# The recurrence's values, the forget gates and the first two heads' queries and keys by Strassen's method, and the forget gates' chain on 64 partitions

## The chip, the core and the metric

The kernel runs on one core of a Trainium2 chip. That core has five engines with queues of their own: TensorE (PE, with its weight loads shown apart as PEld), VectorE (DVE), ScalarE (ACT), GpSimd (POOL) and SyncE (SP), which here issues all transfers. The metric is the time of one execution in microseconds (us); lower is better. The profile is of one execution, and its span runs from the first to the last instruction.

## The reference, cut to what matters

One encoder layer on x of 1024 rows by 1024 features, all in float32:

```python
proj = x @ w_in                      # 1024 x (3*512 + 8 + 4*512 + 2*1024)
q_a, k_a, v_a, f_a, q_b, f_b, i_b, g_b, gate_a, gate_b = split(proj)
log_f = log_sigmoid(f_a + b_f)       # 8 heads; F = cumsum over rows
y_a = fox_attention(...)             # softmax(q k / 8 + F[t] - F[s], s <= t) v, 8 heads of 64
y_b = hgrn2_chunkwise(q_b, 1 - f, i_b, log f)   # 4 heads of 128, state carried over rows
y = sigmoid(gate_a) * (y_a @ w_pa) + sigmoid(gate_b) * (norm(y_b) * ... @ w_pb)
x1 = layer_norm(ALPHA * x + y @ w_o)
out = layer_norm(ALPHA * x1 + swiglu(x1 @ w_ff_in) @ w_ff_out)
```

The change concerns three products with x: `i_b` (the recurrence's values, 512 columns) together with `f_a` (the eight forget gates, 8 columns), and the columns of `q_a` and `k_a` that belong to heads 0 and 1 (128 columns each). It also concerns the cumulative sums of the log forget gates, which every score needs.

## The kernel before, in words

All numbers are float32, and TensorE is given each operand as a high and a low part: ACT casts the high part (`split`: `act.copy`), DVE subtracts it from the source for the low part, and three matmuls (hi·hi, hi·lo, lo·hi: `mm3`) make one product. x is kept transposed, with features on partitions, as four tiles `xh0`, `xh1`, `xl0`, `xl1`. A dot product over 1024 features is eight steps of 128, so 24 matmuls.

The work comes in this order (`Plan` below): the attention's values `va` (the eight PSUM banks hold eight blocks of 128 rows); the recurrence's values with the forget gates, `vb_acc` (eight row blocks, each in two halves of 260 columns, `HV`, so 16 accumulations of 24 matmuls of 260 columns, 384 in all); a transpose of the forget gates (`fps`), a chain of small DVE and ACT steps on 8 partitions by 1024 rows (`fz`, `fa`, `fe`, `fu`: log-sigmoid, then a scan along the rows, then the sums of the odd blocks turned round, since the rows of every second block lie in reverse order); the first pair of heads' queries and keys (`qps`, `kps`, 96 matmuls of 512 columns), whose parts `q2`, `k2`, `kl` ACT and DVE write; and then attention for four pairs of heads, the recurrence's four heads (`bps` and others), the gates, the branch projections `pps`, the output projection `o`, and the feed-forward network (`fa`, `fb`, `fc`, `p`). The box of a head, `box`, holds the cumulative sums of all rows in every partition. It is loaded from `nf_d` in DRAM, POOL adds the causal mask to parts of it, and DVE adds it to the scores `s` while it takes the row maxima (`p<-s,box`).

The order is not that of the code. Each engine call is recorded in `Plan`, a list scheduler with a cost for each call (`Plan.cost`) places the calls one at a time by earliest start and then by rank, and `Plan.issue` sends them out in that order; all instructions therefore bear the line of `getattr(q.engine, method)` in `Plan.issue` (L280). Tiles are slots of a tag with a fixed number of buffers (`BUFS`), handed out first come, first served, so a call also waits for a slot. The gates' plain products (`gps`, weights `wg`, the first eight blocks, `PLAIN`) depend on x alone and are put between other matmuls wherever TensorE would stand still; the remaining gate blocks (`gs`) already use Strassen's method, as does the feed-forward network.

Of the kernel before, what the change touches and what calls it, by code (L numbers as in the profile page):

```python
# [16 lines left out]
P = 128  # L17
# [4 lines left out]
HA, DH = 8, 64  # L22
HB = 4
# [260 lines left out]
def trunk(ctx: ExitStack, tc, a: dict, out: bass.AP):  # L284
# [36 lines left out]
    def const(name, shape, dt=F32):  # L321
        t = keep(shape, name, dt)
        sync.dma_start(t, a[name])
        return t
# [9 lines left out]
    def f(ap):  # L334
        return ap.bitcast(F32)
# [50 lines left out]
    stage = ["qk"] * 6 + ["kb"] * 2  # L386
# [3 lines left out]
    for c2 in range(KC // 2):  # L390
        raws = []
        wraw = take("pf", [2, NB], f"wva{c2}_r")
        for j in range(2):
            raw = full(stage[2 * c2 + j], f"x{2 * c2 + j}_r")
# [25 lines left out]
    causal = const("causal", [P, 2, P], BF16)  # L420
    bf = const("bf", [HA, 1])


    box1 = take("m", [4, S], "box1")
    NV = NB + HA
    HV = NV // 2
    wv = []
    for c in range(KC):
        raw = raw_load(a["w_vb"][c], [NV], f"wvb{c}")
        hi, lo = (full(WTAGS[2 * c + j], f"wvb{c}_{'hl'[j]}", F32R)[:, :NV] for j in range(2))  # L430
        split(hi, lo, raw)
        wv.append((hi, lo))
    vb_d = dram.tile([NT, P, NB], F32, name="vb_d")
    ft = take("gt", [NT, HA], "ft")
    for t in range(NT):
        vb = half(("tt", "ph")[t % 2], f"vb{t}")
        o = [bank(("pt", "h")[t % 2], f"vb_acc{t}_{i}")[:, :HV] for i in range(2)]
        for i in range(2):
            r = slice(i * HV, (i + 1) * HV)
            for c in range(KC):  # L440
                h, l = X(c)
                mm3(o[i], h[:, blk(t)], l[:, blk(t)], wv[c][0][:, r], wv[c][1][:, r], c == 0, c == KC - 1)
        act.copy(vb[:, :HV], o[0])
        dve.tensor_copy(vb[:, HV:], o[1][:, :NB - HV])
        dve.tensor_copy(ft[:, t, :], o[1][:, NB - HV:])
        sync.dma_start(vb_d[t], vb)

    fz, fa, fe, fu = (full("pf", n)[:HA] for n in ("fz", "fa", "fe", "fu"))
# [6 lines left out]
    dve.tensor_scalar(fa, fz, bf, 0.0, op0=ALU.add, op1=ALU.min)  # L455
# [8 lines left out]
    nf = box1[:HA, 2, :]  # L464
    dve.tensor_tensor_scan(nf, fz, fa, 0.0, op0=ALU.add, op1=ALU.subtract)

    nfv, fzv = (t.rearrange("p (j c t) -> p j c t", c=2, t=P) for t in (nf, fz))
    odd = fzv[:, :, 1, :]
    ends = [nfv[:, :, c, P - 1:P].to_broadcast([HA, 4, P]) for c in range(2)]
    dve.tensor_sub(odd[:, :, 1:], ends[1][:, :, 1:], nfv[:, :, 1, :P - 1])  # L470
    dve.tensor_sub(odd[:, :, 0:1], nfv[:, :, 1, P - 1:P], nfv[:, :, 0, P - 1:P])
    dve.tensor_add(nfv[:, :, 1, :], odd, ends[0])
    nf_d = dram.tile([HA, S], F32, name="nf_d")
    sync.dma_start(nf_d, nf)
# [3 lines left out]

    def qk_project(p):
        q2 = [full("qk", f"q2_{p}_{i}", F32R) for i in range(2)]  # L480
        k2 = [full("kb", f"k2_{p}_{i}", F32R) for i in range(2)]
        kl = [full("qk", f"kl_{p}_{i}", F32R) for i in range(2)]
        for b in range(2):
            w = weights(a["w_qk"][b, p], [KC, P], f"w{'qk'[b]}{p}", 0)
            for hf in range(2):
                o = bank("s" if p == 0 else "g", f"{'qk'[b]}ps{p}_{hf}")
                project(o, w, hf)
                for i in range(2):
                    me, ot = slice(i * DH, (i + 1) * DH), slice((1 - i) * DH, (2 - i) * DH)
                    if b == 0:  # L490
                        act.activation(q2[i][me, hs(hf)], o[me], AF.Copy, scale=0.125)
                        dve.scalar_tensor_tensor(q2[i][ot, hs(hf)], o[me], 0.125, f(q2[i])[me, hs(hf)],
                                                 op0=ALU.mult, op1=ALU.subtract)
                    else:
                        act.copy(k2[i][me, hs(hf)], o[me])
                        act.copy(k2[i][ot, hs(hf)], o[me])
                        dve.tensor_sub(kl[i][me, hs(hf)], o[me], f(k2[i])[me, hs(hf)])
                        act.copy(kl[i][ot, hs(hf)], f(kl[i])[me, hs(hf)])
        return q2, k2, kl

    def attention(p, qk):
        q2, k2, kl = qk
        for i in range(2):
# [4 lines left out]
            sync.dma_start(nfx[:, :, 1, :], nf_d[h].rearrange("(j t) -> j t", t=P).partition_broadcast(P))  # L508
# [9 lines left out]
            for qb in range(NT):  # L518
                n = (qb + 1) * P
                pt = full("pf", f"p{h}_{qb}") if qb > 3 else half("ph", f"p{h}_{qb}")  # L520
                mx = small([P, 3], "mx")
# [20 lines left out]
                nm = small([P, 1], "nm")  # L542
# [6 lines left out]
                sm = small([P, 1], "sm")  # L549
                act.activation(pt[:, :n], pt[:, :n], AF.Exp, bias=nm, scale=1.0, accum_out=sm)  # L550
                rs = small([P, 1], "rs")
# [30 lines left out]
    lmask = const("lmask", [P, 2, P], U16)  # L582
# [30 lines left out]
    def hgrn(h, qfg, box):  # L613
# [127 lines left out]
        for hf in range(2):  # L741
            op = bank("pv", f"op{h}_{hf}")
            ss = small([P, 4], "ss")
# [9 lines left out]
            rr = small([P, 4], "rr")  # L753
# [24 lines left out]
    qk = qk_project(0)  # L778
# [16 lines left out]

    def operand4(tags, name):
        ts = [[take(tags[2 * j + i], [2, NB], f"{name}{'hl'[i]}{j}", F32R) for j in range(2)] for i in range(2)]
        return [[ts[i][c // 2][:, c % 2, :] for c in range(4)] for i in range(2)]
# [650 lines left out]
```

## Time and profile before

| what | value |
|---|---|
| time, median of 3 runs | 1476.8 us (1476.67 to 1477.74) |
| profiled execution | 1476.22 us |
| its span | 1474.4 us |
| mean clock granted to TensorE | 0.998 |
| PE, PEld, DVE, ACT, POOL busy | 1455.1, 1208.2, 1053.3, 659.8, 96.6 us |

In the views of the profile a row such as `L280 PE MATMUL vb_acc<-wvb_l,xh 128*128 128x260 f32 x128 | 36.0, 281 | 0.0` stands for 128 matmuls into `vb_acc` of 260 columns: 36.0 us busy in all, 281 ns each, and no idle time before them. Matmuls overlap in the pipeline, so the distance from one start to the next is shorter than the length of one. A row of the timeline gives the start, the length, the engine, the line, the operation and, in brackets, how long the engine had stood idle before and what it waited for. A row of the table by windows gives, for a stretch of time, its length and then the busy time (and number of instructions) of PE, PEld, DVE, ACT and POOL, the granted clock, the share of the DMA engines' time and GB/s.

### The profile page before, as it was taken

How to read it: one execution, taken by the hardware profiler on the slowest of the kernel's cores; microseconds unless marked ns; L12 is line 12 of the kernel's file. 1: busy time of each engine (PE TensorE's matmuls, PEld its weight loads, DVE VectorE, ACT ScalarE, POOL GpSimd, SP SyncE). 2: the span in 40 equal slices, each digit the busy share in tenths (PEclk: the TensorE clock that was granted, in tenths of full speed). 3: DMA queues.
4: the chain of work that ended last, by engine and by line, in shares of the span. 5: the costliest groups of instructions: out<-in, count | busy, mean ns of one | idle time of the engine just before them, and what ended most of it. 6: DMA issues, size and time to landing. Idle time of an engine off the chain costs nothing.

```text
span 1474.4 us, 19347 instructions
## 1 busy us (share of the span) xinstructions
PE 1455.1 (99%) x7033; PEld 1208.2 (82%) x7033; DVE 1053.3 (71%) x1993; ACT 659.8 (45%) x1121; POOL 96.6 (7%) x116
## 2 busy tenths in 40 slices
PE   9999999999999999999999899999999999999998
PEld 7997888888887888788888788888888888888887
DVE  5237676686887899645848897676666666798597
ACT  5126667577568566234611443333333333534430
POOL 0004142130101000000001000000000000000000
PEclk9999999999999999999999999999999999999999
DMA  6202222121211235347610314232222335976741
GB/s 237 78 37 83 58 66 72 47 76 39 73 44 58 86 134 178 119 155 253 225 45 0 115 35 143 100 99 95 95 98 102 107 108 179 342 264 225 258 159 58
DMA packets 79566, 174.86 MB, mean 119 GB/s; under 512 B 7528, under 2 KB 20456, under 8 KB 79472
## 3 DMA queue, kind: packets, MB, share of 16 engines
q1 hardware_dynamic: 79472, 173.64, 34.9%
q8 instruction: 55, 0.90, 0.2%
q14 instruction: 39, 0.32, 0.1%
HBM read 134.52 MB, written 39.09 MB: 118 GB/s over the span
## 4 chain that ended last, share of the span: by engine, by line
PE 93%; DVE 4%; ACT 1%; DMA 1%; issue 0%; POOL 0%; SPq 0%; DVEq 0%; ACTq 0%; POOLq 0%
PE p L280 14%; PE fb L280 11%; PE fc L280 8%; PE fa L280 8%; PE bps L280 8%; PE pps L280 6%; PE o L280 6%; PE gs L280 5%; PE gps L280 5%; PE vb_acc L280 3%; PE va_acc L280 3%; PE kps L280 3%; PE pv L280 2%; PE s L280 2%; PE qps L280 2%; PE pt L280 2%
## 5 line engine op out<-in xcount | busy, mean ns | idle before, releaser
L280 PE MATMUL p<-dp 128*128 128x512 f32 (+1 forms) x957 | 210.0, 382 | 0.0
L280 PEld LDWEIGHTS p<-dp 128*128 128x128 f32 x957 | 175.3, 188 | 34.8
L280 PE MATMUL fc<-xs,Tp 128*128 128x512 f32 x528 | 127.0, 389 | 0.0
L280 PE MATMUL fb<-xs,Tp 128*128 128x512 f32 x528 | 126.7, 389 | 0.0
L280 PE MATMUL fa<-x,Tp 128*128 128x512 f32 x480 | 115.7, 389 | 0.3 <-DVE u L280 0.3
L280 PEld LDWEIGHTS fb<-xs,Tp 128*128 128x128 f32 x528 | 99.1, 188 | 20.6
L280 PEld LDWEIGHTS fc<-xs,Tp 128*128 128x128 f32 x528 | 99.0, 188 | 20.7 <-ACT xs L280 0.2
L280 ACT CAST Tp<-t 128x512 fp32r<-128x512 f32 x88 | 54.3, 620 | 116.2 <-PE fc L280 71.9
L280 PEld LDWEIGHTS fa<-x,Tp 128*128 128x128 f32 x480 | 90.0, 188 | 19.3 <-ACT p L280 0.7
L280 DVE TENSOR_TENSOR Tp<-t,Tp 128x512 fp32r<-128x512 f32 x88 | 60.6, 691 | 60.5 <-ACT Tp L280 60.0
L280 ACT CAST dp<-dap 128x1024 fp32r<-128x1024 f32 (+1 forms) x42 | 41.1, 982 | 99.3 <-PE p L280 45.3
L280 PE MATMUL bps<-xh,wb_l 128*128 128x512 f32 x192 | 76.0, 396 | 0.0
L280 PE MATMUL bps<-xh,wb_h 128*128 128x512 f32 x192 | 75.9, 395 | 0.0
L280 PE MATMUL bps<-xl,wb_h 128*128 128x512 f32 x192 | 75.9, 396 | 0.0
L280 POOL TENSOR_TENSOR rstd<-ve,mhalf 128x1 f32<-128x1 f32 x16 | 14.9, 932 | 887.4 <-DVE ve L280 887.4
L280 DVE TENSOR_TENSOR tl<-pt,th 128x512 fp32r<-128x512 f32 (+1 forms) x96 | 50.7, 552 | 20.3 <-ACT th L280 20.0
L280 DVE TENSOR_TENSOR dp<-dap,dp 128x1024 fp32r<-128x1024 f32 (+1 forms) x42 | 47.5, 1134 | 15.4 <-ACT dp L280 15.4
L280 PE MATMUL fb<-x,Tp 128*128 128x512 f32 x240 | 57.7, 389 | 0.0
L280 POOL TENSOR_SCALAR p<-p,rs 128x128 f32<-128x128 f32 (+3 forms) x64 | 47.5, 749 | 140.7 <-DVE rs L280 91.0
L280 ACT CAST th<-pt 128x512 fp32r<-128x512 f32 (+1 forms) x96 | 43.2, 479 | 28.3 <-PE pt L280 27.1
L280 ACT ACTIVATE p<-p,nm 128x128 f32<-128x128 f32 (+3 forms) x64 | 49.5, 776 | 9.0 <-DVE nm L280 8.5
L280 PEld LDWEIGHTS fb<-x,Tp 128*128 128x128 f32 x240 | 45.1, 188 | 9.4
(374 smaller groups left out, 3511.5 us busy)
## 6 DMA issues: line engine op xcount, KB each, us to landing
dbp<-in_w_fo SPq DMA_DIRECT2D x45, 512.0 KB, 4.8
dap<-a_d SPq DMA_DIRECT2D x35, 512.0 KB, 4.8
a_d<-ar SPq DMA_DIRECT2D x42, 256.0 KB, 3.7
wu_r<-in_w_ff SPq DMA_DIRECT2D x20, 512.0 KB, 3.6
wg_r<-in_w_ff SPq DMA_DIRECT2D x20, 512.0 KB, 3.6
a_d<-as SPq DMA_DIRECT2D x33, 256.0 KB, 2.4
wg_r<-in_w_g SPq DMA_DIRECT2D x16, 512.0 KB, 3.6
sg<-gate_d SPq DMA_DIRECT2D x32, 256.0 KB, 3.5
```

What stands on the lines that cost most here:

```text
L280: getattr(q.engine, method)(*args, **kw)
```

## The change

Strassen's method in Winograd's form multiplies two matrices that are cut in quarters with seven products of quarters instead of eight, and pays with sums of quarters ahead of and behind the products. The change applies it in two places, with the same sums of x (`vops`) in both. With a11, a21 the first 512 features of rows 0 to 511 and of rows 512 to 1023, and a12, a22 the same for the last 512 features, they are p7: a11−a21, p5: a21+a22, p6: p5−a11, p3: a12−p6.

* **Sums of x** (`winograd_sums`). Four sums of four tiles 128x512, on DVE in place in the raw x tiles, and a split of each: 16 sums and 16 subtractions on DVE, 16 casts on ACT. The raw x0 to x3 lie in one tile (`x03_r`, tag "m"), x4 to x7 in "qk".
* **Recurrence's values and forget gates** (`vb_mul`). Seven products into eight banks (`vbx0` to `vbx3`, `vby0` to `vby3`), each of four row blocks, four steps and three matmuls of 260 columns: 336 matmuls. The weights come as four tiles of 128x1040 (`wvb0` to `wvb3`). DVE makes four sums of them, and each product's weights are split as two pieces of 520 columns (`Tvp…`), 14 splits in place of 8. Behind the products stand eight ACT copies and 20 DVE adds of 260 columns into `vbt`, and two DVE copies that gather `ft`. The eight stores `vb_d` go out in pieces of 1 KB per row.
* **Queries and keys of heads 0 and 1** (`qk_first`). Seven products of 12 matmuls of 512 columns (84), on three banks (`qk0_s`, `qk0_pt`, `qk0_s`). The weights are loaded raw (`wq0_r`, `wk0_r`), DVE makes four sums and six combinations of 128x512, ACT two copies, and there are seven splits of 128x512 (`Tqk…`) in place of four. The other three pairs are as before.
* **Forget gates' chain.** One transpose gives `fps` of 64 partitions (block and head) by 128 rows. The chain of steps is the same on 64x128 in place of 8x1024; the sums of the blocks before come from one matmul of one column, `fbase`, with the constant matrix `before`. `nf_d` is now stored by block and head, and the box is loaded from it with another pattern.
* **Tiles.** To make room, the small tiles of the softmax (`mx`, `nm`, `sm`, `rs`) become columns of one, as do two of the recurrence (`ss`, `rr`) and three of the layer norms (`mv`, `ve`, `rstd`), and the masks `causal` and `lmask` take turns in one tile.

```diff
@@ trunk: x raws, sums of x
-    stage = ["qk"] * 6 + ["kb"] * 2
+    xraw = take("m", [4, S], "x03_r")
+    xraws = [xraw[:, c, :] for c in range(4)]
...
+    def sums4(op, dst, x, y, sub):
+        for c in range(4):
+            (dve.tensor_sub if sub else dve.tensor_add)(dst[c], x[c], y[c])
+            split(op[0][c], op[1][c], dst[c])
+
+    vops = {"p1": quarter(0, 0), "p2": quarter(1, 0), "p4": quarter(1, 1)}
+
+    def winograd_sums(ops, raws, tiles):
+        a11, a21, a12, a22 = ([x[:, hs(m)] for x in raws[4 * j:4 * j + 4]] for j, m in ((0, 0), (0, 1), (1, 0), (1, 1)))
+        for name, tile, dst, x, y, sub in (("p7", tiles[2], a11, a11, a21, True), ("p5", tiles[0], a21, a21, a22, False),
+                                           ("p6", tiles[1], a22, a22, a11, True), ("p3", tiles[3], a12, a12, a22, True)):
+            ops[name] = tile()
+            sums4(ops[name], dst, x, y, sub)
@@ trunk: recurrence's values and forget gates
-    for t in range(NT):
-        vb = half(("tt", "ph")[t % 2], f"vb{t}")
-        o = [bank(("pt", "h")[t % 2], f"vb_acc{t}_{i}")[:, :HV] for i in range(2)]
-        for i in range(2):
...
-                mm3(o[i], h[:, blk(t)], l[:, blk(t)], wv[c][0][:, r], wv[c][1][:, r], c == 0, c == KC - 1)
...
+    def vb_mul(p, src, o, first):
+        lane = lane_of(None)
+        T = [[take(f"w{x}{lane}", [2, HV], f"Tv{p}{x}{j}", F32R) for j in range(2)] for x in "hl"]
+        for j in range(2):
+            split(T[0][j], T[1][j], src[:, 2 * j:2 * j + 2])
...
+        for t in range(4):
+            for c in range(4):
+                mm3(o[t][:, :HV], A[0][c][:, blk(t)], A[1][c][:, blk(t)], T[0][c // 2][:, c % 2], T[1][c // 2][:, c % 2],
+                    first and c == 0, c == 3, more)
...
+    vb_mul("p1", b11, vx, True)
+    for t in range(4):
+        act.copy(p1v[:, t], vx[t][:, :HV])
+    vb_mul("p2", b21, vx, False)
+    vb_out(0, 0, act.copy, vx)
+    dve.tensor_sub(b12, b12, b11)
+    dve.tensor_sub(t2, b22, b12)
+    vb_mul("p6", t2, vy, True)
+    vb_out(0, 1, dve.tensor_add, vy, p1v)
+    vb_mul("p5", b12, vx, True)
...
+    vb_mul("p3", b22, vx, False)
+    vb_out(1, 0, dve.tensor_add, vy, p1v)
...
@@ trunk: forget gates' chain
-    for hf in range(2):
-        fps = bank("s", f"fps{hf}")
-        for t in range(4):
-            tr(fps[:HA, blk(t)], ft[:, 4 * hf + t, :], ident)
-        dve.tensor_copy(fz[:, hs(hf)], fps[:HA])
-    act.activation(fe, fz, AF.Abs, bias=bf, scale=1.0)
+    fps = bank("h", "fps")[:BH, :P]
+    tr(fps, ft.rearrange("p t h -> p (t h)"), ident)
+    f4 = half("gt", "f4")[:BH]
+    fz, fa, fe, fu = (f4[:, blk(i)] for i in range(4))
+    act.activation(fe, fps, AF.Abs, bias=bf, scale=1.0)
...
+    base = bank("h", "fbase")[:BH, :1]
+    mm(base, before[:, :BH], nf[:, P - 1:P], start=True, stop=True)
+    dve.tensor_sub(fz, fz, fa)
+    dve.tensor_scalar(fz, fz, before[:, BH + 1:BH + 2], base, op0=ALU.mult, op1=ALU.add)
+    dve.scalar_tensor_tensor(nf, nf, before[:, BH:BH + 1], fz, op0=ALU.mult, op1=ALU.add)
+    nf_d = dram.tile([NT, HA, P], F32, name="nf_d")
...
@@ qk_first, called in place of qk_project(0)
+        def mul(p, src, o, first):
+            T = [take(f"w{x}0", [4, P], f"Tqk{p}{x}", F32R) for x in "hl"]
+            split(*T, src)
+            more = {} if first else {"skip_group_check": True}
+            for c in range(4):
+                mm3(o, T[0][:, c], T[1][:, c], vops[p][0][c], vops[p][1][c], first and c == 0, c == 3, more)
+
+        mul("p1", b11, oa, True)
+        act.copy(p1, oa)
+        mul("p2", b21, oa, False)
+        dve.tensor_sub(b12, b12, b11)
+        dve.tensor_sub(t2, b22, b12)
+        qk_heads(0, 0, oa, *tiles)
+        mul("p6", t2, ob, True)
+        dve.tensor_add(u2, ob, p1)
+        mul("p5", b12, oc, True)
...
```

The planner sets the new order. On TensorE, at the end of the recurrence's values, there stands before (`vb_acc7_1` is the second half of the last row block, `qps0_0` the first half of the queries):

```order
L280 MATMUL vb_acc7_1_161<-wvb7_l_135,xh1_67 128x260
L280 MATMUL vb_acc7_1_161<-wvb7_h_134,xl1_69 128x260
L280 MATMUL fps0_166<-ident_108,ft_137 8x128 x4
L280 MATMUL fps1_167<-ident_108,ft_137 8x128 x3
L280 MATMUL qps0_0_190<-xh0_66,wq0_h0_186 128x512
L280 MATMUL fps1_167<-ident_108,ft_137 8x128
L280 MATMUL qps0_0_190<-xl0_68,wq0_h0_186 128x512
L280 MATMUL qps0_0_190<-xh0_66,wq0_l0_187 128x512
```

and in the changed kernel (`vbx3` is the last bank of product p3, `gps0_0_0` a plain gate product):

```order
L281 MATMUL vbx3_138<-Tvp3l1_170,vs4h3_121 128x260
L281 MATMUL vbx3_138<-Tvp3h1_168,vs4l3_125 128x260
L281 MATMUL gps0_0_0_1120<-xh0_66,wg0_0_h0_1116 128x512
L281 MATMUL gps0_0_0_1120<-xl0_68,wg0_0_h0_1116 128x512
L281 MATMUL qk0_s_191<-xh0_66,Tqkp1h_200 128x512
L281 MATMUL qk0_s_191<-xl0_68,Tqkp1h_200 128x512
L281 MATMUL gps0_0_0_1120<-xh0_66,wg0_0_l0_1117 128x512
L281 MATMUL qk0_s_191<-xh0_66,Tqkp1l_201 128x512
```

Gate products that stood behind the queries and keys now stand between them, and the one transpose stands eight rows further on, no longer right behind the recurrence's values.

On DVE, at the end of the attention's values, there stands before (`wvb…_l` are the low parts of the recurrence's weights, `wq0_l…` those of the first queries, and the copies take the finished banks of `va`):

```order
L280 TENSOR_TENSOR wvb5_l_129<-wvb5_r_127,wvb5_h_128 128x520
L280 TENSOR_TENSOR wvb6_l_132<-wvb6_r_130,wvb6_h_131 128x520
L280 TENSOR_TENSOR wvb7_l_135<-wvb7_r_133,wvb7_h_134 128x520
L280 TENSOR_TENSOR wq0_l0_187<-wq0_r_185,wq0_h0_186 128x512
L280 TENSOR_TENSOR wq0_l1_189<-wq0_r_185,wq0_h1_188 128x512
L280 COPY va_107<-va_acc0_71 128x512
L280 TENSOR_TENSOR wg0_0_l0_1302<-wg0_0_r_1300,wg0_0_h0_1301 128x512
L280 COPY va_107<-va_acc2_73 128x512
```

and in the changed kernel (`x4_r` to `x7_r` hold the sums by then, `vs4` is the operand of p3, `Tvp1` the weights of p1):

```order
L281 TENSOR_TENSOR vs4l2_124<-x6_r_98,vs4h2_120 128x512
L281 TENSOR_TENSOR x7_r_99<-x7_r_99 128x512
L281 TENSOR_TENSOR Tvp1l0_145<-wvb0_r_128,Tvp1h0_143 128x520
L281 TENSOR_TENSOR wvb1_r_129<-wvb1_r_129,wvb0_r_128 128x1040
L281 TENSOR_TENSOR vs4l3_125<-x7_r_99,vs4h3_121 128x512
L281 TENSOR_TENSOR Tvp1l1_146<-wvb0_r_128,Tvp1h1_144 128x520
L281 TENSOR_TENSOR lbt_182<-lbl_181 128x4
L281 RECIPROCAL lbt_182<-lbt_182 128x4
L281 TENSOR_TENSOR lbt_182<-lbt_182 128x4 x2
L281 TENSOR_SCALAR lbt_182<-lbt_182 128x4
L281 COPY va_104<-va_acc0_72 128x512
```

All sums of x and their low parts now stand ahead of the first bank's copy, and the splits of the recurrence's weights, but for those of p1, behind it.

On DVE, in the stretch of the first queries and keys, there stands before (`f…` are the steps of the forget gates' chain, `q2` the scaled queries, `wk0_l0` a low part of the keys' weights):

```order
L280 TENSOR_SCALAR fu_165<-fe_164 8x1024
L280 TENSOR_SCALAR fu_165<-fu_165 8x1024
L280 SCALAR_TENSOR_TENSOR q2_0_0_179<-qps0_0_190,q2_0_0_179 64x512
L280 TENSOR_TENSOR fe_164<-fe_164,fu_165 8x1024
L280 SCALAR_TENSOR_TENSOR q2_0_1_180<-qps0_0_190,q2_0_1_180 64x512
L280 TENSOR_TENSOR fe_164<-fe_164,fu_165 8x1024
L280 TENSOR_TENSOR wk0_l0_194<-wk0_r_192,wk0_h0_193 128x512
L280 TENSOR_TENSOR fz_162<-fz_162,fe_164 8x1024
```

and in the changed kernel (`f4` is the chain's tile, `Tqk…l` the low parts of the products' weights, `wq0_r` and `wqk_t2` sums of weights):

```order
L281 TENSOR_TENSOR Tqkp2l_203<-wq0_r_186,Tqkp2h_202 128x512
L281 COPY ft_127<-vbt_134 128x8x4
L281 TENSOR_TENSOR wq0_r_186<-wqk_t2_188,wq0_r_186 128x512
L281 COPY ft_127<-vbt_134 128x8x4
L281 TENSOR_TENSOR wq0_r_186<-wq0_r_186,wqk_t2_188 128x512
L281 TENSOR_SCALAR f4_173<-fps_172,bf_107 64x128
L281 TENSOR_SCALAR f4_173<-f4_173 64x128
L281 TENSOR_TENSOR Tqkp6l_205<-wqk_t2_188,Tqkp6h_204 128x512
L281 TENSOR_SCALAR f4_173<-f4_173 64x128
L281 TENSOR_TENSOR f4_173<-f4_173 64x128
L281 TENSOR_TENSOR wg0_0_l1_1119<-wg0_0_r_1115,wg0_0_h1_1118 128x512
```

The chain's steps now stand between weight sums and splits of the seven products, no longer between the queries' evacuations.

More of the change, by code (lines that the diff above doesn't have):

```diff
@@ L22 @@
 HA, DH = 8, 64
+HV = 260
 HB = 4
@@ L419, in trunk @@
     ident = const("ident", [P, P])
[L420 to L432, printed above, removed]
+    causal = const("causal", [P, 2, P], BF16, "mask")
+    bf = const("bf", [NT * HA, 1])
@@ new lines, in quarter @@
+    def quarter(i, m):
+        return [[x[i][:, c, hs(m)] for c in range(4)] for x in (xh, xl)]
+    def sums4(op, dst, x, y, sub):
[9 more added lines that the diff above has]
+            sums4(ops[name], dst, x, y, sub)
@@ L485, in qk_project @@
             for hf in range(2):
-                o = bank("s" if p == 0 else "g", f"{'qk'[b]}ps{p}_{hf}")
+                o = bank("g", f"{'qk'[b]}ps{p}_{hf}")
                 project(o, w, hf)
[L488 to L498, printed above, removed]
```

166 lines of the change are left out of this document (114 added, 52 removed).

## The prediction

> **What bounds the kernel now.** I read the page's shares first, then the chain that ended last.
>
> ```profile
> span 1474.4 us, 19347 instructions
> PE 1455.1 (99%) x7033; PEld 1208.2 (82%) x7033; DVE 1053.3 (71%) x1993; ACT 659.8 (45%) x1121; POOL 96.6 (7%) x116
> PE 93%; DVE 4%; ACT 1%; DMA 1%; issue 0%; POOL 0%; SPq 0%; DVEq 0%; ACTq 0%; POOLq 0%
> ...
> 8.13 41.78 PE va_acc L280 x183
> 49.91 45.55 PE vb_acc L280 x384
> ...
> 224.99 10.88 PE kps L280 x48
> ```
>
> TensorE carries 93% of the chain, and the whole of the recurrence's values is one piece of it. Since a busy TensorE need not run at its pace, I take the pace from pieces: 384 matmuls of 260 columns in 45.53 us (next table) are 118.6 ns each, 48 of 512 columns in 10.88 us are 226.7 ns. So a matmul removed there is worth its full pace, provided that TensorE is given other work without a gap. The stages show who could be late instead.
>
> ```profile
> core 0: us, PE busy (x) PEld busy (x) DVE busy (x) ACT busy (x) POOL busy (x), PEclk, DMA share, GB/s
> 8.13:49.75 41.62, 41.62 (x184) 34.47 (x184) 23.50 (x34) 20.77 (x31) 0.00 (x0) 1.00 0.58 198
> 49.75:95.28 45.53, 45.53 (x385) 45.51 (x384) 4.35 (x16) 4.12 (x10) 0.00 (x0) 1.00 0.15 53
> 95.28:97.06 1.78, 1.78 (x14) 1.42 (x12) 1.57 (x4) 1.14 (x2) 0.00 (x0) 1.00 0.15 58
> 97.06:114.08 17.02, 15.45 (x68) 12.13 (x66) 13.89 (x18) 7.78 (x10) 0.00 (x0) 1.00 0.03 11
> 114.08:120.44 6.36, 6.36 (x29) 5.32 (x30) 2.04 (x4) 3.59 (x7) 0.00 (x0) 1.00 0.45 147
> 120.44:300.00 179.56, 179.38 (x944) 146.42 (x943) 128.10 (x452) 124.62 (x267) 54.58 (x66) 1.00 0.22 65
> 300.00:571.25 271.25, 268.46 (x1428) 224.17 (x1428) 223.91 (x503) 182.97 (x325) 26.95 (x30) 1.00 0.24 78
> ```
>
> The first row is the attention's values (DVE idle 18 of 42 us), the second the recurrence's (DVE and ACT all but idle), the third to fifth the transposes and the first queries and keys (TensorE 1.6 us short, DVE at 82% in the middle one), the last two attention and recurrence. The clock is full throughout, so no term needs a correction for it. Two waits matter:
>
> ```profile
> PE fa L280 <- ACT Tp_0h L280: 4.1, 1, 4.1
> ...
> PE kps L280 <- DVE wk_l L280: 1.6, 2, 1.3
> ```
>
> The first lies in the feed-forward network, where the change alters nothing. The second is a key-weight split held up in DVE's queue behind the forget gates' chain on 8 partitions; below I count it as removed.
>
> **The change part by part, TensorE.** The recurrence's values fall from 384 to 7·4·4·3 = 336 matmuls: 48·118.6 ns = −5.69 us. Queries and keys of the first pair fall from 96 to 84: 12·226.7 ns = −2.72 us. The transposes:
>
> ```profile
> 95.28 0.93 PE L280 MATMUL fps<-ident,ft 128*8 128x128 f32 x7
> 95.97 0.48 PE L280 MATMUL qps<-xh,wq_h 128*128 128x512 f32 x1
> 96.28 0.27 PE L280 MATMUL fps<-ident,ft 128*8 128x128 f32 x1
> 96.31 0.48 PE L280 MATMUL qps<-xl,wq_h 128*128 128x512 f32 x1
> ```
>
> Seven take 95.97−95.28 = 0.69 us; with the eighth, started 0.03 us ahead of its successor, about 0.7. In their place come one transpose, about 0.1 (a seventh of 0.69), and the one-column float32 matmul `fbase`. No float32 matmul with a single column is in the trace; between the 0.1 of a transpose and the 0.27 of one's whole length I take 0.15. Net −0.45, between −0.3 and −0.6.
>
> The kps wait of 1.57 us goes: the splits of the last products are issued behind a chain whose steps are eight times shorter in free size (128 columns for 1024). What is late next there is the split of product n+1 behind the evacuation of product n; against it the new order lays 16 gate matmuls, 3.6 us, among the 84. I charge 0.6 us of new stalls, for one or two hand-overs; bounds 0 (all covered by gate products) and 3 (half of seven hand-overs at the 0.8 that the two kps waits had on average).
>
> Sum: −5.69−2.72−0.45−1.57+0.6 = −9.8 us.
>
> A rule of the Trainium skill speaks against the second term: "TensorE: Matmul & The Clock Gate", section Back-to-back issue gap, gives about 131 ns per matmul of 512 columns in a sustained stream of weight loads and matmuls, and 81 ns for 128. By it, 12 matmuls would be 1.57 us, and an estimate halfway for 260 columns, 98 ns, would make 4.7 of the first term; the sum would be −7.7. This trace disagrees, with 226.7 and 118.6 ns per matmul over 48 and 384 in a row, each with its own weight load, so the measurement decides.
>
> **What must stay hidden.** The x sums go under the attention's values, where DVE and ACT have these prices:
>
> ```profile
> L280 DVE TENSOR_TENSOR xl<-x_r,xh 128x1024 fp32r<-128x1024 f32 x7 | 8.6, 1225 | 2.5 <-ACT xh L280 2.1
> L280 DVE TENSOR_TENSOR wvb_l<-wvb_r,wvb_h 128x520 fp32r<-128x520 f32 x8 | 5.6, 699 | 5.4 <-ACT wvb_h L280 5.4
> L280 DVE TENSOR_TENSOR wva_l<-wva_r,wva_h 128x512 fp32r<-128x512 f32 x7 | 4.7, 688 | 2.5 <-ACT wva_h L280 2.5
> L280 ACT CAST wvb_h<-wvb_r 128x520 fp32r<-128x520 f32 x8 | 5.0, 624 | 5.8 <-DMA wvb_r<-in_w_vb 5.8
> L280 ACT CAST wva_h<-wva_r 128x512 fp32r<-128x512 f32 x7 | 4.3, 621 | 4.2 <-PE va_acc L280 2.4 <-DVE wvb_l L280 1.2 <-DMA wva_r<-in_w_va 0.5
> L280 ACT COPY vb<-vb_acc 128x260 f32<-128x260 f32 x8 | 3.0, 376 | 39.0 <-PE vb_acc L280 39.0
> L280 DVE COPY vb<-vb_acc 128x252 f32<-128x252 f32 x7 | 2.9, 421 | 35.1 <-PE vb_acc L280 35.1
> ...
> L279 ACT ACT_TABLE_LOAD x1 | 1.3, 1283 | 0.0
> ...
> 45.19 0.69 DVE L280 COPY va<-va_acc 128x512 f32<-128x512 f32 x1 [3.75 <-PE va_acc L280]
> ```
>
> DVE gets 16 sums and 16 low parts at 0.688: +22.0 us. Out of the stage go eight splits of 0.699 (−5.6) and the query and gate splits (four of 0.688, −2.8); in come p1's two (+1.4) and one weight sum of 1040 columns (+1.25, by the 1225 ns of 1024). 23.5+22.0−5.6−2.8+1.4+1.2 = 39.7 of 41.6 us, including 2.8 of copies of `va`. That is tight. The work ahead of the first copy, some 37 us from the first split on, ends at 45 to 46.5; the copy moves from 45.19 to about 47; TensorE wants bank 0 and p1's weights at 49.75. The slack is about 3 us, and I cost the sums at nothing; with that cover gone, each further microsecond is one of TensorE. ACT, with 20.8+16·0.621−5.0+1.2 = 26.9 of 41.6, has room, also for the two more table loads that the new order gives it (1.28 each).
>
> Under the recurrence's values (39.8 us now) DVE gets 12 splits of 0.699 (8.4), three further weight sums of 1040 columns (3.7), and up to 20 adds of 260 columns, at the 421 ns of a copy of 252 about 8.4: 20.5 of 40 us. ACT gets 12·0.624+8·0.376 = 10.5. Each product lasts 48·118.6 ns = 5.7 us, while the next product's split, two casts and two low parts, needs 2.6 in two lanes of buffers, so it is ready some 3 us ahead. The weights' four loads carry the bytes of eight; the stores come later, far ahead of their readers.
>
> The merges order columns that were written and read in sequence anyway. One wait is new: SP's load of `lmask` stands until POOL's last use of `causal`, and stores of `ya` and the recurrence's first weights queue behind it.
>
> ```profile
> 271.20 2.29 POOL L280 TENSOR_TENSOR box<-box,causal 128x512 f32<-128x512 f32 x2
> ...
> 285.53 11.69 SPq L280 DMA_DIRECT2D wb_r<-in_w_b  x2
> ```
>
> That use ends at 273.5, and the weights behind it are issued at 285.5, so it is hidden by 12 us; nothing.
>
> The first scores also need the box:
>
> ```profile
> 109.73 2.28 DVE L280 TENSOR_TENSOR_SCAN box<-fz,fa 8x1024 f32<-8x1024 f32 x1
> 114.14 0.68 DVE L280 TENSOR_TENSOR box<-fz,box 8x512 f32<-8x512 f32 x1
> 121.95 4.54 POOL L280 TENSOR_TENSOR box<-box,causal 128x512 f32<-128x512 f32 x4 [121.50 <-DMA box<-nf_d]
> 123.41 0.27 DVE L280 CUSTOM_DVE_ANT_0 p<-s,box 128x128 f32<-128x128 f32 x1
> ```
>
> Its chain lasted from the transposes at 95.28 to 114.8, and POOL began 7.1 us after it. A step of 128 columns costs at most the 0.27 of the last row, against 0.68 to 2.28; twelve on DVE, four on ACT and their hand-overs I put at 6 us from 92.5. Then the masked box is there at 98.5+7.1+4.5 = 110, and no longer the last to come.
>
> In the queries-and-keys stage DVE is the tight one. Behind the last vb product (49.75+39.8 = 89.6) stand 4 adds (1.7), two gathers, 7 low parts (4.8), the remaining 2 weight sums (1.4), 6 combinations and 8 head parts at 0.69 (9.7), 2 gate splits (1.4), two `vhl` (1.3) and the twelve chain steps (2.4, at 0.2 each, below that 0.27): some 23 us of work, up from 17.5 in rows three to five. TensorE needs 84·0.227+16·0.227 = 22.7 us, until 112.6, so the two run level.
>
> **Rivals.** *B, scores come less early than the matmuls do.* From 89.6, DVE's 23 us end at 112.6 without a wait, at about 116 with 3.5 us of them (the row from 97.06 has 3.1 in 17). The first reduction then starts some 7.3 us before its 123.41, not 9.8. TensorE covers the difference with gate products; but these are finite:
>
> ```profile
> core 0: us, PE busy (x) PEld busy (x) ACT busy (x), PEclk, DMA share, GB/s
> ...
> 120.40:300.00 179.60, 42.96 (x140) 24.61 (x140) 2.98 (x5) 1.00 0.22 65
> 300.00:571.30 271.30, 64.92 (x244) 44.14 (x244) 5.86 (x10) 1.00 0.24 78
> ```
>
> All 384 of them are spent between 120 and 571 us, and DVE is at 83% in the second stretch. If the attention and recurrence were bound by their chain, the gain would be that of the first score, −7.3, or −5 with some stalls after spent fillers: 1469.5 to 1471.5. Against it: TensorE is idle only 3 of 451 us there.
>
> *C, the opening is late.* If the x sums run 5 to 12 us past my 46, TensorE waits 2 to 9 us at 49.75, or in the last steps of the values for x's low parts: about 1475, same within a measurement.
>
> *D, slower: seven exposed hand-overs in `qk_first`.* If no split is ready ahead, TensorE waits in each product for an evacuation (0.69, as the copy of `va`), a cast (0.62) and a low part (0.69), 2.0 us: 14 us against the 9.8 gained, so 1481. It decides at 9.8/7 = 1.4 us each. For it: DVE's queue is full there, and one stall of that kind stands in the trace (kps). Against it: two buffers of `Tqk` and gate matmuls in between.
>
> **How the numbers follow.** What a measurement can tell from no change is 0.2%, 2.95 us. The profiled execution took 1476.22 (span 1474.4 and 1.8 around it), 0.6 below the median; I take −9.8 from its span, 1464.6, and from the median, 1467.0. Forecast 0.64, with its own range of 1464 to 1469.5: no new stalls and the transposes at their best give −10.6, and −12.6 if the network's 4.1 were halved by chance of order; 3 us of stalls give −7.3. B 0.24, C 0.06, D 0.06. Faster is all of the forecast and B, with a little of C: 0.90; same 0.04; slower D: 0.06. The range, 1464 to 1471.5, holds the forecast and B.
>
> **What would show it.** Right: matmuls into `vbx` and `vby` back to back, 39.8 us from about 49.8; no wait of TensorE on DVE above 1 us before 115; first reduction at 113 to 117; gate work `gs` starting some 10 us earlier than 571. B shows as a `gs` start only 5 to 7 us earlier, with more idle time before `bps`, `s` or `pt`; C as a wait of the first `vbx` on `Tvp1` or on a copy of `va`; D as waits of `qk0` on `Tqk` of over 1 us each. It would be wrong outright if the sums' prices, from rows of other tiles, were higher in place, or if the new order made the attention's waits grow by more than the 9.8.

## The result: slower, and the loss is not where the change is

| | time, us | ratio to before |
|---|---|---|
| before | 1476.74 (1476.37 to 1477.74) | |
| changed | 1488.95 (1487.89 to 1490.04) | 1.0082, 95% interval 1.0064 to 1.0099 |

The changed kernel takes 12.2 us more, where 9.8 us less was forecast. The page of the changed kernel, as far as it answers to the lines shown of before:

```profile
span 1486.1 us, 19300 instructions
PE 1466.9 (99%) x6968; PEld 1201.4 (81%) x6968; DVE 1090.0 (73%) x2051; ACT 675.8 (45%) x1150; POOL 98.2 (7%) x116
PE 91%; DVE 5%; ACT 1%; DMA 1%; issue 1%; POOL 0%; SPq 0%; DVEq 0%; ACTq 0%; POOLq 0%
```

TensorE is still busy 99% of the time and carries the chain, with fewer matmuls and more microseconds. Its waits in the stretch that the change rewrote are small (waits of the changed kernel from 85 to 125 us: who waits for whom, total, times, longest):

```profile
PE s L281 <- DVE soft L281: 0.6, 1, 0.6
PE qk_pt L281 <- DVE qk_p L281: 0.3, 1, 0.3
```

So no new wait took the time. The chain shows where it went (start, length, what, count; the changed kernel first, then two pieces of before that were not shown yet):

```profile
8.05 42.81 PE va_acc L281 x183
50.86 11.55 PE vbx L281 x96
...
166.23 11.17 PE kps L281 x48
...
648.70 89.18 PE pps L281 x384
...
1269.00 209.91 PE p L281 x957
```

```profile
649.23 87.04 PE pps L280 x384
...
1257.54 209.88 PE p L280 x957
```

Pieces whose matmuls no line of the diff touches take longer: 183 matmuls of the attention's values 42.81 us for 41.78, 48 of `kps` 11.17 for 10.88, 384 of `pps` 89.18 for 87.04. For the last two, which lie far from anything that was edited, that is 232 to 233 ns for 512 columns in place of 226.7. The last stage alone, `p`, takes what it took. Windows of 350 us in the feed-forward network say the same, 1512 matmuls for 1546 (before, then changed):

```profile
core 0: us, PE busy (x) PEld busy (x) DVE busy (x) ACT busy (x) POOL busy (x), PEclk, DMA share, GB/s
900.00:1250.00 350.00, 350.00 (x1546) 289.91 (x1545) 239.01 (x361) 110.59 (x184) 0.00 (x0) 1.00 0.33 109
```

```profile
900.00:1250.00 350.00, 350.00 (x1512) 284.35 (x1511) 235.75 (x358) 106.95 (x181) 0.00 (x0) 1.00 0.32 104
```

The granted clock is 1.00 in both windows, and no idle time is recorded in them. Where one matmul of 512 columns follows another within 260 ns, ahead of the last stage, the mean from start to start is 231.8 ns (4277 matmuls) for 227.4 before (4299): 19 us. The 48+12 matmuls saved are worth less than half of it.

What differs in the same matmul is where its operands lie. The weights of the recurrence with their gate columns, 260 wide, make two kinds of slots longer: those of the lanes `wh`, `wl` from 2048 to 2080 bytes (`Tv…`, 2x260 numbers), those of `wr` and `kb` from 4096 to 4160 (`wvb…`, 4x260 numbers). All tiles behind them move. Start addresses of the slots that TensorE reads, per partition, modulo 256 bytes, from the built programs:

```
tag          before         changed
x            32             64
wh0, wl0     32             64, 96, 128, 160
wh1, wl1     32             192, 224, 0, 32
wr0, wr1     32             64, 128
kb           32             192, 0, 64, 128
pf qk v hl ph tt   32       64
```

Before, the stationary operand lay at the same address modulo 256 as the moving operand, but for 24 matmuls with a constant and for half of the recurrence's values, which were 16 bytes off and ran no slower (118.6 ns in both halves). With each matmul of the changed kernel's trace given its two addresses from the built program, the pace goes by their difference (ns from start to start for 512 columns, as above; the moving operand's address less the stationary one's; the first six matmuls of a run with one difference, and the later ones):

```
difference mod 256   first six        later
0                    231.1 (x901)     227.1 (x398)
32                   232.1 (x160)
64                   233.1 (x312)     232.2 (x154)
96                   232.5 (x239)
128                  232.3 (x460)     233.5 (x148)
160                  232.1 (x242)
192                  233.1 (x538)     233.0 (x294)
224                  232.5 (x410)
```

Only at a difference of 0 does a run of matmuls settle at the old pace, after some six of them (in the kernel before, too, the first six behind an interruption take 231.1 ns). In the last stage both operands lie in one tile, and its pace is whole. This gave the theory that the runs test, called "phase" below; its rival, "work", is that the sums, splits and the new order slow TensorE through traffic in SBUF.

### The profile page after: what moved, and what is told of

Its sections match the earlier page's. It is cut to its first block, busy times and chain, and to the rows that moved or that the text cites. A ratio compares the mean times of both kernels' runs of the same rounds, so it can differ in the third digit from the quotient of the medians.

```text
span 1486.1 us, 19300 instructions
## 1 busy us (share of the span) xinstructions
PE 1466.9 (99%) x6968; PEld 1201.4 (81%) x6968; DVE 1090.0 (73%) x2051; ACT 675.8 (45%) x1150; POOL 98.2 (7%) x116
## 4 chain that ended last, share of the span: by engine, by line
PE 91%; DVE 5%; ACT 1%; DMA 1%; issue 1%; POOL 0%; SPq 0%; DVEq 0%; ACTq 0%; POOLq 0%
PE p L281 14%; PE fb L281 12%; PE bps L281 8%; PE fa L281 8%; PE fc L281 8%; PE pps L281 6%; PE o L281 6%; PE gs L281 5%; PE gps L281 4%; PE va_acc L281 3%; PE kps L281 2%; PE pv L281 2%; PE qps L281 2%; PE pt L281 2%; PE vbx L281 2%; PE lp L281 1%
## 5 line engine op out<-in xcount | busy, mean ns | idle before, releaser
L281 ACT CAST Tp<-t 128x512 fp32r<-128x512 f32 x88 | 54.3, 619 | 119.9 <-PE fc L281 74.6
L281 POOL TENSOR_TENSOR norm<-norm,mhalf 128x1 f32<-128x1 f32 x16 | 14.6, 912 | 894.2 <-DVE norm L281 894.2
L281 POOL TENSOR_SCALAR p<-p,soft 128x128 f32<-128x128 f32 (+3 forms) x64 | 48.3, 760 | 123.2 <-DVE soft L281 106.4
L281 ACT ACTIVATE p<-p,soft 128x128 f32<-128x128 f32 (+3 forms) x64 | 49.6, 775 | 11.6 <-DVE soft L281 10.5
L281 DVE TENSOR_TENSOR u<-fb,p 128x512 f32<-128x512 f32 x44 | 30.4, 691 | 33.0 <-PE fb L281 32.9
```

The lines of the kernel that those rows point to most:

```text
L281: getattr(q.engine, method)(*args, **kw)
```

## Experiments

**Half width 256.** One number of the change is taken back, the four gate columns per half, which restores every slot's length.

```diff
-HV = 260
+HV = 256
...
-        dve.tensor_copy(ft[:, :, 4 * n:4 * n + 4], vbt[:, :, n, NB // 2:])
+        dve.tensor_copy(ft[:, :, 4 * n:4 * n + 4], vbt[:, :, n, HV - 4:])
```

> The changed kernel with 256 in place of 260 columns per half (HV = 256): the four gate columns of each half are left out of the product, and the forget gates' chain works on the last value columns instead, so the forget gates are not those of the reference. The planner's order and all counts stay, but no tile is longer than its old slot, and all slots of SBUF again start at the same address modulo 512 bytes. Theory 'phase' (TensorE keeps its pace of 227 ns per 512 columns only where its stationary and its moving operand lie at the same address modulo 256 bytes): the pace of 232 goes back to 226.7 ns, some 4000 matmuls by 5.3 ns, 20 us: 1466 to 1470 us. Rival 'work' (the sums, splits and the new order slow TensorE through traffic in SBUF): 1486 to 1489 us, pace 232.

1469.08 us (1468.25 to 1469.67), ratio to before 0.9946 (0.993 to 0.9963). The same 384 `pps` matmuls and the 48 `kps`:

```profile
164.85 10.88 PE kps L281 x48
...
642.45 87.04 PE pps L281 x384
```

All of Strassen's work but the gate columns is in this kernel, and TensorE has its old pace and its gain. "Work" falls; 19.9 us come back.

**Nothing but addresses.** Three kernels have the instructions of before and an unused pad: of 128 and of 256 bytes between the buffers of x and all others, and of 128 bytes ahead of all.

```diff
     xl = [take("x", [4, S], f"xl{i}", F32R) for i in range(2)]
+    plan.tile(root, [P, 32], F32, "pad", "pad", 1)
```

> The kernel before, with an unused pad of 128 bytes between the five buffers of tag x and all other tiles; no instruction changes. Phase: every matmul with one operand in x and the other elsewhere loses its pace, until the last stage, which has both in x; 15 to 21 us slower, 1492 to 1498 us, pace 232 ns per 512 columns, last stage at 226.7. Work: 1476.8 us, nothing changes.

> The same with a pad of 256 bytes (and two buffers fewer of a 4-byte tile of the layer norms, to make room). Phase, modulo 256: 1477 us within 2, pace 226.7 to 227.5. If the modulus is 512 or more: 1492 to 1498 us. Work: 1477.

> The kernel before with the pad of 128 bytes ahead of all large tiles, so that all move together. Phase (the difference of the two addresses matters): 1476.8 us within 1.5. Rival 'absolute' (each address by itself must be aligned): 1488 us or more, pace 232. Work: 1476.8.

| pad | time, us | ratio to before |
|---|---|---|
| 128 behind x | 1492.29 (1491.34 to 1493.44) | 1.0106 (1.009 to 1.0121) |
| 256 behind x | 1476.71 (1475.75 to 1477.68) | 0.9999 (0.999 to 1.0009) |
| 128 ahead of all | 1476.35 (1474.78 to 1478.27) | 0.9998 (0.9989 to 1.0007) |

An idle pad of 128 bytes costs 15.4 us. The chain of that kernel:

```profile
167.54 11.15 PE kps L280 x48
...
654.34 87.05 PE pps L280 x384
...
1272.90 210.14 PE p L280 x957
```

`kps`, with one operand in x, has lost its pace. `pps` and `p`, whose two operands were moved together or not at all, have kept it. In this trace, runs at a difference of 128 stay at 233.0 ns after their first six matmuls (2266 of them), those at 0 reach 226.8 (764). A pad of 256, or one that moves both operands, changes nothing. So the difference counts, modulo 256 bytes, and neither address by itself. All three issue the instructions of before in the same order on every engine.

**Lanes only.** The split is taken a step of 260 columns at a time, so that the lane slots are 2048 bytes again; `wr` and `kb` stay at 4160.

```diff
-        for t in range(4):
-            for c in range(4):
+        for c in range(4):
+            hi, lo = (take(f"w{x}{c % 2}", [HV], f"Tv{p}{x}{c}", F32R) for x in "hl")
+            split(hi, lo, src[:, c])
+            for t in range(4):
...
```

> The changed kernel with only the eight lane slots (wh, wl) back at 2048 bytes, by splits one step of 260 columns at a time; the slots of wr and kb stay at 4160, so that four of the six slots of the feed-forward network's weights remain out of phase. Phase: pace 226.7 up to the output projection and a mean near 231 in the network's chunks; about two thirds of 1776 matmuls by 5.3 ns, 6 us, above the aligned kernel: 1473 to 1477 us. Work: as the changed kernel, 1487 to 1490.

1477.06 us (1476.0 to 1478.57), ratio 1.0004 (0.9995 to 1.0013): 11.9 us below the changed kernel, at the upper edge of what was expected. `kps` is back at 10.88 us, and the network, whose weights lie in `kb` and `wr`, is not:

```profile
core 0: us, PE busy (x) PEld busy (x) DVE busy (x) ACT busy (x) POOL busy (x), PEclk, DMA share, GB/s
900.00:1250.00 350.00, 350.00 (x1517) 284.91 (x1516) 235.87 (x357) 109.23 (x182) 0.00 (x0) 1.00 0.33 107
```

1517 matmuls, 230.7 ns each. The loss therefore splits into about 12 us of the lanes and 9 of `kb` and `wr`. The latter is above the 6 expected. In this window the two thirds out of phase take 232.4 ns, and the third in phase 228.0, since each product of twelve matmuls spends its first few on settling; over the network's 1776 matmuls that makes 7.5 us, and the rest lies ahead of the network.

**The whole change, in phase.** This keeps the gate columns and all of the change, and brings the other slots back as well: the gate columns of the raw quarters lie in a tile of their own, and p1's copy waits in its place in the output tile.

```diff
+    wvg = keep([P, 5, 4, 4], "wvg")
+    sync.dma_start(wvg[:, :4], a["w_vg"])
...
-        t = take(tag, [4, HV], f"wvb{i}_r")
+        t = take(tag, [4, NV], f"wvb{i}_r")
...
-    p1v = take("kb", [4, HV], "vb_p1")
     vbt = take("m", [NT, 2, HV], "vbt")
+    p1v = vbt[:, 4:, 0, :]
...
+            split(hi[:, :NV], lo[:, :NV], src[0][:, c])
+            split(hi[:, NV:], lo[:, NV:], src[1][:, c])
```

> The whole change, with every large slot of SBUF again a multiple of 256 bytes: the weights' split is taken one step of 260 columns at a time into the slots of 2048 bytes, the products run step by step over their four row blocks, the four gate columns of each raw quarter lie in a tile of their own, and p1's copy waits in its place in the output tile. 336 and 84 matmuls as in the change; 28 splits in two pieces each instead of 14, and four small sums more. Phase: 1467 to 1470 us, pace 226.7. Work: the finer splits and more small steps on DVE and ACT stall TensorE in the recurrence's values, 1472 to 1480 us.

1468.20 us (1466.96 to 1468.77), ratio 0.9942 (0.993 to 0.9955). It is faster than both kernels: 8.5 us below before, 20.8 below the changed one. `kps` takes 10.88 us, and the recurrence's matmuls have 118.6 ns (the changed kernel had 120.3):

```profile
49.43 11.39 PE vbx L282 x96
...
161.83 10.88 PE kps L282 x48
...
640.14 87.04 PE pps L282 x384
```

**Plain queries and keys.** The aligned kernel without `qk_first`.

```diff
-    qk = qk_first()
+    qk = qk_project(0)
```

> The aligned kernel with the first pair's queries and keys as before (96 matmuls in place of 84, four splits in place of seven, no sums or combinations). By the prediction's terms: 2.7 us slower than the aligned kernel. By rival B (DVE holds up the first scores): the first reduction comes as early or earlier, and the time is within 1 us of the aligned kernel or below it.

1471.32 us (1469.34 to 1473.52), ratio 0.9965 (0.9952 to 0.9979): 3.1 us above the aligned kernel, where the matmuls alone make 2.7. The first reduction comes at 115.68 us, 0.7 before that of the aligned kernel, as rival B had it, but the time does not follow it. The waits of TensorE on `wk_l` do not come back with the plain splits, but one takes their place:

```profile
PE s L282 <- DVE soft L282: 3.2, 1, 3.2
```

Right behind this wait the clock granted to TensorE is at half for 3.4 us:

```profile
116.93:120.34 3.41, 3.41 (x10) 2.62 (x9) 2.45 (x15) 3.32 (x9) 0.86 (x2) 0.50 0.47 154
```

The aligned kernel's longest wait on `soft` is 1.3 us, with no such stretch behind it. The 3.1 us are thus a sum of several things, the wait and some 1.7 us of lost clock among them, and their nearness to 2.7 confirms nothing.

**Small tiles apart.** The aligned kernel with the softmax's and the recurrence's small tiles as before.

```diff
-                soft = small([P, 6], "soft")
-                mx, nm, sm, rs = soft[:, :3], soft[:, 3:4], soft[:, 4:5], soft[:, 5:]
+                mx, nm, sm, rs = small([P, 3], "mx"), small([P, 1], "nm"), small([P, 1], "sm"), small([P, 1], "rs")
```

> The aligned kernel with the softmax's four small tiles and the recurrence's two apart again, as in the kernel before. If the merges cost nothing, as predicted: the aligned kernel's time within 0.7 us. If the merged tile holds up the row maxima (the changed kernel's profile names it in 1.1 us of TensorE's waits): 1 to 2 us faster.

1474.93 us (1473.91 to 1477.64), ratio 0.9991 (0.9982 to 1.0): 6.7 us slower, which neither expectation had. Its waits and its chain name a cause outside the tiles:

```profile
PE pt L282 <- POOL p L282: 4.9, 1, 4.9
```

```profile
124.96 9.24 DMA box<-nf_d
```

The planner's order for this kernel puts the masking of the second head's box ahead of a scaling of `p` in POOL's queue, and that box took 9.2 us to land. Behind the wait the clock is again at half, for 5.7 us of work, which adds some 2.9 us in this execution (1476.48 us):

```profile
136.65:142.39 5.74, 5.74 (x17) 4.57 (x17) 2.21 (x4) 1.56 (x3) 3.54 (x5) 0.50 0.47 140
```

The DMA issues from 90 to 300 us (tile, count, KB each, median us to landing) of before and of the changed kernel:

```profile
box<-nf_d SPq DMA_DIRECT2D x8, 512.0 KB, 4.2
```

```profile
box<-nf_d SPq DMA_DIRECT2D x8, 512.0 KB, 8.9
```

The same bytes take twice as long since the change: `nf_d` lies by block and head, so a box is eight pieces of 512 bytes 4 KB apart in DRAM, not one run of 4 KB. Four kernels test this.

**Scattered boxes in the kernel before.** Only the layout of `nf_d` changes.

```diff
-    nf_d = dram.tile([HA, S], F32, name="nf_d")
-    sync.dma_start(nf_d, nf)
+    nf_d = dram.tile([NT, HA, P], F32, name="nf_d")
+    sync.dma_start(nf_d.rearrange("t h p -> h t p"), nf.rearrange("h (t p) -> h t p", p=P))
...
-            sync.dma_start(nfx[:, :, 1, :], nf_d[h].rearrange("(j t) -> j t", t=P).partition_broadcast(P))
+            sync.dma_start(nfx[:, :, 1, :], nf_d[:, h, :].partition_broadcast(P))
```

> The kernel before with nf_d laid out in DRAM as in the change (by block, then head): only the store and the eight box loads change their pattern. Scattered box: landing 8 to 9 us, POOL waits for most boxes, 1 to 4 us slower than the kernel before (1477.5 to 1481 us). Traffic: landing 4.2, no change.

1483.41 us (1482.72 to 1483.62), ratio 1.0047 (1.0035 to 1.006): 7.1 us slower, more than expected. The landing time is 8.9 us as in the changed kernel, and a new wait stands at the top of TensorE's list:

```profile
box<-nf_d SPq DMA_DIRECT2D x8, 512.0 KB, 8.9
```

```profile
PE s L280 <- DVE mx L280: 4.6, 1, 4.6
```

The order of the instructions is that of before. Here too half the clock follows the wait, for 3.0 us of work, so that 4.6 us of waiting cost some 6.1; a further wait of `pt` on POOL has 0.9:

```profile
127.90:130.93 3.03, 3.03 (x8) 2.55 (x9) 2.22 (x11) 0.98 (x4) 0.72 (x1) 0.50 0.45 143
```

**Boxes by rows in the aligned kernel**, merged and apart: the 64 partitions go by head and then block.

```diff
-    nf_d = dram.tile([NT, HA, P], F32, name="nf_d")
-    sync.dma_start(nf_d.rearrange("t h p -> (t h) p"), nf)
+    nf_d = dram.tile([HA, NT, P], F32, name="nf_d")
+    sync.dma_start(nf_d.rearrange("h t p -> (h t) p"), nf)
```

> The aligned kernel with the forget gates' chain ordered by head and then block on its 64 partitions (in place of block and head), so that nf_d lies in DRAM by head and row, as in the kernel before, and a head's box is read from one run of 4 KB instead of eight pieces of 512 bytes 4 KB apart. Theory 'scattered box' (the landing time of a box, 8.7 us in the changed kernel's median against 4.2 before, comes from that layout and costs attention 1 to 4 us, as POOL waits for 7 or 8 of the 8 boxes): landing back to 4 to 5 us, POOL waits for 2 or 3, 1464 to 1467 us. Rival 'traffic' (the boxes are late because other loads now run beside them): landing stays near 8.7, 1468 us.

> The same with the softmax's and the recurrence's small tiles apart again. In the unmerged aligned kernel TensorE stood 4.9 us behind POOL, which stood behind a box that took 9 us to land, and the time was 6.7 us above the merged one. Scattered box: with boxes that land in 4 to 5 us this wait is gone and the time is within 1.5 us of the run beside it. Rival (the tiles apart cost time by themselves): again 5 us or more above it.

In both kernels the boxes land in 4.1 to 4.2 us. Merged: 1471.43 us (1470.38 to 1473.6), ratio 0.9968 (0.9956 to 0.9981), 3.2 us above the aligned kernel although the transfers are faster, where 1464 to 1467 was expected. Apart: 1469.25 us (1468.89 to 1469.96), ratio 0.9952 (0.9936 to 0.9967); the wait of 4.9 us is gone, and the tiles apart are now within 1.1 us of the aligned kernel, though 2.2 below the merged run beside it, where 1.5 at most was expected. The merged one has another order than the aligned kernel, since its two gathers of the gates no longer depend on each other for the planner. The next run removes that difference.

**Boxes by rows in the same order.** The two heads' groups interleave on the 64 partitions, so that every instruction keeps its place in the aligned kernel's order.

```diff
-    ft = take("gt", [HA, NT], "ft")
+    ft = take("gt", [4, 2, NT], "ft")
...
-            sync.dma_start(nfx[:, :, 1, :], nf_d[h].partition_broadcast(P))
+            sync.dma_start(nfx[:, :, 1, :], nf_d[2 * (h % 4) + h // 4].partition_broadcast(P))
```

> The aligned kernel with the box layout by head and row, and with every instruction in the order of the aligned kernel (the two heads' groups interleave on the 64 partitions, so that the two gathers of the gates keep their dependency, and the planner its order). If the box's landing time costs the changed kernel something: landing 4.1 instead of 8.7 us, and 1 to 4 us below the aligned kernel's 1468.2. If this order hides it: 1467.5 to 1469 us, and the 3.2 us between the aligned kernel and the one by rows came from the planner's other order alone.

1467.34 us (1466.92 to 1468.15), ratio 0.9937 (0.9924 to 0.9951), with boxes in 3.8 us. Beside the aligned kernel's 0.9942 this is no difference: in this order the slow boxes were hidden. So scattered boxes cost 6 to 7 us, half clock included, where the planner has put something that TensorE needs behind one, and nothing where it has not, and the 3.2 us of the run before it came from the order. In that run `ot` waits 2.8 us on `ob`, 0.7 in the aligned kernel; the rest was not traced.

## Why the prediction was wrong

**The step that failed** is the one that took the pace from pieces of before, 118.6 and 226.7 ns, and let it stand: "The clock is full throughout, so no term needs a correction for it." The clock was no different: in both kernels it is at half for 3.4 us behind the wait of `fa` at about 835 us, beyond the rows that the prediction read, and otherwise full. But the pace was a property of the addresses as well, and the change moved them. Some 4200 matmuls that no line of the diff touches were priced at no change; by their pace they cost 19 us, and with everything in phase the changed kernel's time falls by 20.8. The sum was made over edited instructions only; the lengths of the slots (2x260 numbers in a lane of 2x256) stood in the diff and were not followed to the tiles behind them. None of the rivals came near: C and D looked for waits, and the loss has none.

**The terms themselves**, judged on the aligned kernel, where the pace is that of before:

* *Sum, −9.8.* Measured −8.5 (0.9942), at the upper end of the forecast's own range.
* *Recurrence's values, −5.69.* 96 matmuls in 11.39 us are 118.6 ns each, so this term is right. *Queries and keys, −2.72.* Not measured by itself: the plain kernel's 3.1 holds its wait and its half clock as well.
* *The kps wait goes.* Right, but with the plain queries and keys a wait of `s` on `soft` of 3.2 us comes in its place, so of the 7.7 us summed for the values, the transposes and this wait, 5.3 us were measured in that kernel (1476.66 to 1471.32), its half clock included. The sum named the split of product n+1 as what is late next; it was the first scores.
* *New stalls of 0.6.* 0.9 in the changed kernel between 85 and 125 us, both waits shown above; 1.3 in the aligned one, a wait of `s` on `soft`.
* *The opening's cover.* DVE was reckoned at 39.7 of 41.6 us and at 20.5 under the recurrence's values. Measured in the changed kernel:

```profile
core 0: us, PE busy (x) PEld busy (x) DVE busy (x) ACT busy (x) POOL busy (x), PEclk, DMA share, GB/s
8.05:50.86 42.81, 42.81 (x185) 34.67 (x186) 38.13 (x59) 24.84 (x39) 0.00 (x0) 1.00 0.40 156
50.86:91.30 40.44, 40.44 (x337) 40.44 (x337) 20.71 (x38) 11.43 (x22) 0.00 (x0) 1.00 0.25 79
```

No matmul into `vbx` waits, so rival C falls, and with no wait of `qk` above 0.3 us rival D falls too.

* *First scores.* The first reduction was looked for at 113 to 117 us (changed kernel, then aligned):

```profile
119.42 0.29 DVE L281 CUSTOM_DVE_ANT_0 p<-s,box 128x128 f32<-128x128 f32 x1
```

```profile
116.41 0.29 DVE L282 CUSTOM_DVE_ANT_0 p<-s,box 128x128 f32<-128x128 f32 x1
```

Aligned, it comes 7.0 us earlier than before, as rival B had it (7.3), and the end comes 8.5 us earlier, between B and the forecast. The first `gs` starts at 557.54 us for 571.25, 13.7 earlier, where B had 5 to 7: gate products did fill the gap.

* *The box.* That a transfer can become slower by its pattern was missed: 8.9 us for the 4.2 of before. In the aligned kernel's order it was hidden; the forecast had no ground to count on it.
* *The merges cost nothing.* Not settled. Apart, the tiles were 6.7 us slower with scattered boxes and 2.2 faster with boxes by rows, and the order changed with them each time; the lowest time of all, 1467.34, is of merged tiles.
* *Prices in place.* The low parts of the keys, `kl`, were reckoned at 0.69 us. Beside POOL's masking of the box two of them took 1.34 and 1.30 (last section), in the stage where DVE was the tight engine; how much of the first reduction's time that makes was not measured.
* *Two slips of working.* TensorE's 22.7 us behind 89.6 end at 112.3, not 112.6, and −5 from the median is 1471.8, not 1471.5. Neither changes the forecast.

The rule weighed in the prediction, about 131 ns per matmul of 512 columns in a sustained stream ("TensorE: Matmul & The Clock Gate", Back-to-back issue gap, of the Trainium skill), is as far off here as before: the measured pace was 226.7 ns in phase and 232 to 233 out of it.

## What to carry to other kernels

When an edit changes the size of any tile, list the start addresses of all buffers that TensorE reads before and after, and keep stationary and moving operands at the same address modulo 256 bytes, here by padding or by splitting the odd part off. When many untouched matmuls of a trace are each a few nanoseconds longer at a full clock, compare addresses before looking for waits. Price a transfer by its pattern as well as by its bytes, and ask what the planner has put behind it, since the same slow boxes cost 7 us in one order and nothing in another.

## What the runs showed of the hardware

* Matmuls of 512 columns (fp32r, a weight load of 128 columns each) run at 226.7 ns when the two operands' addresses agree modulo 256 bytes and at 232 to 233 ns when they differ by 32 to 224. The agreement takes about six matmuls to show, and 24 matmuls with a constant 132 bytes off kept 226.6 ns inside runs that were in phase. With 260 columns the mean is 118.6 ns in phase and 120.3 in the changed kernel, but the rule is less clean: in the kernel with the pad of 128 bytes, those at 128 took 119.9 and those at 144 took 118.4. What in the reads of SBUF makes it so was not settled: only the addresses were varied, not the size of the weight load or the type.
* A narrower matmul need not be shorter: 256 columns, in phase, took 119.9 ns (96 in the row below), 260 columns 118.6.

```profile
49.95 11.51 PE vbx L281 x96
```

* Loads of 512 KB that spread 4 KB of DRAM over 128 partitions landed in 3.8 to 4.2 us when the 4 KB were one run and in 8.7 to 8.9 when they were eight pieces of 512 bytes.
* The granted clock was at half for 3.4 to 6.8 us behind every wait of TensorE of 3.2 us or more in these traces (the rows from 116.93, 127.90 and 136.65 us above), and behind none of up to 1.7 us.
* POOL's masking of a box took 1.17 us per half before and 1.37 in the aligned kernel, where it falls beside DVE's `kl` (two halves in 2.74). DVE's row is longer too: the same `kl` took 0.68 us just ahead of the masking and 1.34 beside it:

```profile
108.80 2.74 POOL L282 TENSOR_TENSOR box<-box,causal 128x512 f32<-128x512 f32 x2 [108.36 <-DMA box<-nf_d]
```

```profile
107.57 0.68 DVE L282 TENSOR_TENSOR kl<-qk_pu,k 64x512 fp32r<-64x512 f32 x1
...
109.18 1.34 DVE L282 TENSOR_TENSOR kl<-qk_pu,k 64x512 fp32r<-64x512 f32 x1
110.79 1.30 DVE L282 TENSOR_TENSOR kl<-qk_p,k 64x512 fp32r<-64x512 f32 x1 [0.27 <-ACT k L282]
```

The Trainium skill ("SBUF — State Buffer", Who interferes with whom) says that a VectorE instruction with two SBUF inputs contends with a GpSimd instruction that reads SBUF, which is the case here: `qk_pu` and `k` both lie in SBUF. The trace agrees, with both engines slower, and no run varied it alone.
